# A stationary matmul form rewritten as three 256-column products a step, in a one-core encoder layer

## The chip, the cores and the metric

The kernel runs on one core of one Trainium2 chip. The metric is the device time of one execution in microseconds; lower is better. Engines are named as in the profile: PE is TensorE (matmuls), PEld its weight loads, DVE VectorE, ACT ScalarE, POOL GpSimd and SP SyncE, which here issues nearly all DMAs.

## The reference

One layer of an encoder on 256 tokens of width 2048, in float32:

```
h = rmsnorm(x, g_mix)
proj = einsum('bsd,de->bse', h, w_in)
q_a, k_a, v_a, q_r, f_fwd, f_bwd, i_r, g_r, gate_a, gate_r = split_columns(proj)
...
y_attn = einsum('bse,ed->bsd', bidirectional_gqa(q_a, k_a, v_a), w_o_attn)
o_r = hgrn2_bidirectional(q_r, f_fwd, f_bwd, i_r, g_r, lb, g_hgrn)
y_hgrn = einsum('bse,ed->bsd', o_r, w_o_hgrn)
mixed = sigmoid(gate_a) * y_attn + sigmoid(gate_r) * y_hgrn
x = x + einsum('bsd,de->bse', mixed, w_out)
h = rmsnorm(x, g_mlp)
u = square(relu(einsum('bsd,df->bsf', h, w_up)))
x = x + einsum('bsf,fd->bsd', u, w_down)
ple_gate = sigmoid(einsum('bsd,de->bse', rmsnorm(x, g_ple), w_ple_gate))
x = x + ple_gate * einsum('bsc,cd->bsd', p, w_ple)
return rmsnorm(x, g_final)
```

The attention has 16 query and 4 key heads of 128, with a norm and a rotation of queries and keys. The second branch is a gated linear recurrence with 16 heads, in both directions: `q_r` passes through a SiLU, `f_fwd` and `f_bwd` through a sigmoid. The hidden width of the MLP is 8192.

## The kernel before

**Precision.** Every large product is made of three: an operand is split into a rounded part hi and a remainder lo, both of type float32r, and hi x hi, hi x lo and lo x hi are summed in PSUM. For the weights, `prep_half` makes hi on ACT (line 112) and lo on DVE (line 113), half a tile of 128x1024 at a time. The activations lie in SBUF as `[128, 8, 2, 256]` tiles: for each 128-row block `k` of the inner dimension first the 256 tokens of hi, then those of lo. `xs(X, k)` is such a block, `[128, 2, 256]`.

**Weights.** All weights stream through in a fixed list, `order`, as tiles of 1 MB. `next_w` hands out the next tile, and puts the load of the tile two ahead on SP's queue and the split of the tile one ahead on ACT and DVE.

**Two forms of product.** `gemm_mov` has the activations stationary and the weights moving, 512 columns a product (line 207); it serves most projections. `gemm_st` has the weights stationary and the activations moving, so that results come out transposed; it serves the recurrence's `q_r`, `f_fwd` and `f_bwd` (48 tiles of 128 output features) and the MLP's up-projection (64). It works on two output tiles at once, `e` = 0 and 1, each with a PSUM tile of 512 columns, over 16 blocks `k`. For each `k` the weights' hi part meets both parts of the activations in one product of 512 columns (line 181), and the lo part meets the hi part of the activations in one of 256 (line 184), which adds onto the first 256 columns. The PSUM tile then holds two partial results side by side, and `merge` adds them: ACT copies the second half to SBUF (line 189), DVE adds the first half to it (line 190). What follows reads that sum: a SiLU for `q`, a sigmoid for each forget gate (line 617), and in the MLP the square of the ReLU (line 699).

**Order of the work.** Smaller chains (attention, the scan of the recurrence, the transposes of results) are Python generators. `tick` advances a clock by the time that each group of products is expected to take, and when it reaches a generator's due time, the generator's next piece is put between the large products. So `yield 7.0` means: go on after 7 us of large products. `attend` begins with `heads_T`, which squares each head of the projected queries (line 398), normalizes and rotates them (the last addition on line 414), waits for `pause`, transposes them on TensorE (line 421) and splits the result into `qT` (lines 424 and 425); then come the scores (line 449), the transposes of the probabilities (line 480) and the products with the values (line 469). In the scan, ACT copies keys (line 527) for products on line 535. The engines' queues run in order.

**Start.** SP loads the first quarter of `x` in two pieces of 256 KB, each followed by half of the first weight tile (lines 291 and 292), and then the other quarters and tiles in turn. ACT and DVE split them (lines 303 to 309), and the first large products follow.

Of the kernel before, what the change touches and what calls it, by code (L numbers as in the profile page):

```python
# [7 lines left out]
AF = mybir.ActivationFunctionType  # L8
ALU = mybir.AluOpType
# [3 lines left out]
P = 128  # L13
D = 2048
S = 256
KT = D // P
# [10 lines left out]
def build(tc, xT, xtok, pT, gains, gfin_in, ropet, ident_in, masks_in, ghg_in, lb_in,  # L27
# [41 lines left out]
    with contextlib.ExitStack() as es:  # L69
# [14 lines left out]
        def nm(s):  # L84
            cnt[0] += 1
            return f"{s}_{cnt[0]}"
# [4 lines left out]
        def gps():  # L91
            return psg.tile([P, 512], F32, tag="g", name=nm("g"))
# [66 lines left out]
        def wsl(w, k, n):  # L159
            per = 1024 // n  # L160
            t = w[k // per]
            o = (k % per) * n
            return t[:, o:o + n]
# [5 lines left out]
        def gemm_st(arr, b, X, last=None):  # L169


            ps = [gps() for _ in range(2)]
            for c in range(2):
                his, los = next_w((arr, b + c))
                for kk in range(KT // 2):
                    k = KT // 2 * c + kk
                    if k == 12 and last:
                        last()
                    x = xs(X, k)
                    for e in range(2):  # L180
                        pe.matmul(ps[e], wsl(his, 2 * kk + e, P), x, start=k == 0, stop=False)  # L181
                    tick(0.33)
                    for e in range(2):
                        pe.matmul(ps[e][:, :S], wsl(los, 2 * kk + e, P), x[:, 0, :], start=False, stop=k == KT - 1)  # L184
                    tick(0.33)
            return ps

        def merge(ps, z):
            act.activation(z, ps[:, S:], AF.Copy)
            dve.tensor_tensor(z, ps[:, :S], z, ALU.add)  # L190
            return z

        def gemm_mov(arr, j, X, last=None, stagger=False):

# [91 lines left out]
        dve.memset(nhalf, -0.5)  # L286
        act.dma_start(gn, gains)
        raws[0] = wraw.tile([P, 2048], F32, tag="raw", bufs=3, name=nm("raw"))
        for a in range(2):
            w2 = slice(1024 * a, 1024 * a + 1024)  # L290
            sp.dma_start(xf[:, 2 * a:2 * a + 2], xT[:, 2 * a:2 * a + 2])
            sp.dma_start(raws[0][:, w2], w_mov[order[0][1:]][:, w2])
        for i in range(1, 4):
            sp.dma_start(xf[:, 4 * i:4 * i + 4], xT[:, 4 * i:4 * i + 4])
# [144 lines left out]
        SC = HD ** -0.5  # L439

        def attend(j, ps):
            qT = yield from heads_T(ps, 0, "qT", 7.0 if j else 10.0)
            probs, pts = {}, {}
            for i in range(6):
                if i < 4:
                    sc = mps()
                    for t in range(NT):
                        for n, (a, b) in enumerate(TERMS):
                            pe.matmul(sc[:, t * S:(t + 1) * S], qT[:, i, a, t * P:(t + 1) * P], kT[:, j, b],  # L449
                                      start=n == 0, stop=n == 2)  # L450
                    mx = t1([P, NT], "mx", 2)
                    dve.tensor_reduce(mx, sc.rearrange("p (t s) -> p t s", t=NT), AX.X, ALU.max)
                    dve.tensor_scalar(mx, mx, -SC, None, ALU.mult)
                    pr = com.tile([P, NT, S], F32, tag="yb", bufs=2, name=nm("pr"))
                    sm = t1([P, NT], "sm", 2)
                    for t in range(NT):
                        act.activation(pr[:, t], sc[:, t * S:(t + 1) * S], AF.Exp, bias=mx[:, t:t + 1], scale=SC,
                                       accum_out=sm[:, t:t + 1])
                    dve.reciprocal(sm, sm)
                    for t in range(NT):  # L460
                        dve.tensor_scalar(pr[:, t], pr[:, t], sm[:, t:t + 1], None, ALU.mult)
                    probs[i] = pr
                    yield 1.5
                if 0 <= i - 2 < 4:
                    pt = pts.pop(i - 2)
                    av = mps()
                    for s in range(NT):
                        for n, (a, b) in enumerate(TERMS):
                            pe.matmul(av[:, :S], va[:, s, a, j * HD:(j + 1) * HD], pt[:, s, b],  # L469
                                      start=s == n == 0, stop=s == NT - 1 and n == 2)  # L470
                    o = xs(OA, 4 * j + i - 2)
                    act.activation(o[:, 0, :], av[:, :S], AF.Copy)
                    dve.tensor_tensor(o[:, 1, :], av[:, :S], o[:, 0, :], ALU.subtract)
                    yield 1.5
                if 0 <= i - 1 < 4:
                    pr = probs.pop(i - 1)
                    tp = mps()
                    for s in range(NT):
                        for t in range(NT):
                            pe.transpose(tp[:, s * S + t * P:s * S + (t + 1) * P], pr[:, t, s * P:(s + 1) * P], ident)  # L480
                    pt = t1([P, NT, 2, S], "pt", 1, F32R)
                    tv = tp.rearrange("p (s t) -> p s t", s=NT)
                    act.activation(pt[:, :, 0], tv, AF.Copy)
                    dve.tensor_tensor(pt[:, :, 1], tv, pt[:, :, 0], ALU.subtract)
                    pts[i - 1] = pt
                yield 3.0
# [24 lines left out]
        def scan_head(h, q, T, vi, gg):  # L511
# [16 lines left out]
                return kc  # L528

            kc = keys(1)  # L530
            yield 7.0
            for li, L in enumerate(LEVELS):
                pl = mps()
                for t in range(NT):
# [54 lines left out]
        for j in range(4):  # L589
            ps = proj(f"i{j}", Hm) if j else ps_i0  # L590
            vi = t2([P, NT, 512], "vi")
            for t in range(NT):
                act.activation(vi[:, t], ps[t], AF.Copy)
            ps = proj(f"g{j}", Hm)
            gg = t2([P, NT, 512], "gg")
            for t in range(NT):
                act.activation(gg[:, t], ps[t], AF.Sigmoid)
                dve.tensor_tensor(gg[:, t], ps[t], gg[:, t], ALU.mult)
                g4 = gg[:, t].rearrange("p (h v) -> p h v", h=4)
                pool.tensor_tensor(g4, g4, ghg.unsqueeze(1).to_broadcast([P, 4, HD]), ALU.mult)  # L600
            pend = []
            for h in range(4 * j, 4 * j + 4):
                for a in range(3):
                    if not pend:
                        pend = gemm_st("st", 3 * h + a, Hm)
                    ps = pend.pop(0)
                    if a == 0:
                        q = t2([P, S], "q")
                        sg = t2([P, S], "sg")
                        merge(ps, q)  # L610
                        act.activation(sg, q, AF.Sigmoid)
                        dve.tensor_tensor(q, q, sg, ALU.mult)
                        T = t2([P, 2, S], "T1")
                        continue
                    d = a - 1
                    merge(ps, T[:, d])
                    act.activation(T[:, d], T[:, d], AF.Sigmoid)
                    dve.tensor_scalar(T[:, d], T[:, d], oml[:, d, h:h + 1], low[:, d, h:h + 1], ALU.mult, ALU.add)  # L618
                weave(scan_head(h, q, T, vi, gg))

# [56 lines left out]
        for step in MLP:  # L677
            c = int(step[1])
            if step[0] == "u":
                pend = []  # L680
                for f in range(16):
                    if not pend:
                        pend = gemm_st("up", c * 16 + f, H1, last=flush if c == f == 0 else None)
                    ps = pend.pop(0)
                    if c == f == 0:
                        st3.close()
                        ph4, st4 = open_pool("ph4", side="right")

                        def t4(shape, tag, bufs=2, dt=F32):
                            return ph4.tile(shape, dt, tag=tag, bufs=bufs, name=nm(tag))  # L690

                        row_r(0)
                        dve.tensor_tensor(r1s, rr[0], rr[0], ALU.mult)
                        UA = [bigt(F32R, [P, 8, 2, S]) for _ in range(2)]
                        UB = [t4([P, 8, 2, S], f"UB{i}", 1, F32R) for i in range(2)]
                        t4([P, 120], "pad", 1)
                    r = merge(ps, t4([P, S], "r"))
                    uu = t4([P, S], "uu")
                    dve.scalar_tensor_tensor(uu, r, 0.0, r, ALU.max, ALU.mult)
                    u = xs(UA if c % 2 == 0 else UB, f)  # L700
                    act.activation(u[:, 0, :], uu, AF.Copy)
                    dve.tensor_tensor(u[:, 1, :], uu, u[:, 0, :], ALU.subtract)
                continue
# [161 lines left out]
```

## Time and profile before

| | |
|---|---|
| median of 3 runs | 1979.24 us (1978.99 to 1980.14) |
| the profiled execution | 1979.2 us |
| its span in the trace | 1977.3 us |
| TensorE busy | 1955.2 us, 99% |
| VectorE busy | 1227.8 us, 62% |
| ScalarE busy | 950.6 us, 48% |
| DMA | 358.59 MB, 181 GB/s on average |

The span is the time from the first to the last instruction of the program; the execution's own time has 1.9 us more. The ends of matmuls are modelled in the trace, and successive matmuls overlap, so what a product costs is read from start to start.

### The profile page before, as it was taken

The numbers are of one execution on the slowest core, as the hardware profiler recorded it, in microseconds if no ns is written. First come the engines' busy times: TensorE is split into PE (matmuls) and PEld (weight loads), VectorE is DVE, ScalarE is ACT, GpSimd is POOL, SyncE is SP. The second block draws the span as 40 slices with busy tenths as digits, with TensorE's granted clock in tenths as the row PEclk, the third lists the DMA queues.
The fourth block names the chain that finished last, engine by engine and source line by source line (L and its number), as shares of the span: only waits on it lengthen the run. The fifth ranks groups of instructions, "written<-read, shape, count | busy, mean of one in ns | idle before, by whom it ended". The sixth has DMA issues, their size and how long they took to land.

```text
span 1977.3 us, 25896 instructions
## 1 busy us (share of the span) xinstructions
PE 1955.2 (99%) x9996; PEld 1659.1 (84%) x9996; DVE 1227.8 (62%) x1756; ACT 950.6 (48%) x1512; POOL 109.6 (6%) x161
## 2 busy tenths in 40 slices
PE   8999999999999999999999999999999999999998
PEld 6788888888888888888888888888888888888886
DVE  6877687686785884545545566665466455545555
ACT  6676554454554553434434454443344344434544
POOL 0000021110210110000000000000000000000001
PEclk9999999999999999999999999999999999999999
DMA  8534444544444445555565555555555555555552
GB/s 332 181 132 146 149 158 145 183 146 158 171 145 157 168 147 175 190 194 189 192 234 197 192 175 189 190 192 191 192 192 192 192 192 192 192 192 190 203 197 113
DMA packets 51676, 358.59 MB, mean 181 GB/s; under 512 B 5984, under 2 KB 6240, under 8 KB 9056
## 3 DMA queue, kind: packets, MB, share of 16 engines
q1 hardware_dynamic: 50832, 355.85, 50.3%
q8 instruction: 79, 1.29, 0.2%
q10 hardware_dynamic: 720, 1.08, 0.1%
q14 instruction: 45, 0.37, 0.1%
HBM read 354.81 MB, written 2.10 MB: 180 GB/s over the span
## 4 chain that ended last, share of the span: by engine, by line
PE 92%; DVE 1%; ACT 1%; issue 1%; POOLq 0%; POOL 0%; ACTq 0%; DVEq 0%
PE g L207 55%; PE g L181 20%; PE g L184 10%; PE m L535 3%; PE m L469 1%; PE g L732 1%; PE m L238 1%; PE m L449 1%; PE m L570 0%; PE m L569 0%; PE m L480 0%; PE m L555 0%; ACT hi L112 0%; DVE lo L113 0%; PE m L561 0%
## 5 line engine op out<-in xcount | busy, mean ns | idle before, releaser
L113 DVE TENSOR_TENSOR lo<-raw,hi 128x1024 fp32r<-128x1024 f32 x658 | 805.1, 1243 | 634.8 <-ACT hi L112 600.1
L112 ACT ACTIVATE hi<-raw 128x1024 fp32r<-128x1024 f32 x658 | 677.8, 1055 | 795.6 <-PE g L207 461.1
L207 PE MATMUL g<-hi,big 128*128 128x512 f32 (+1 forms) x2720 | 665.6, 391 | 8.0 <-ACT hi L303 8.0
L207 PEld LDWEIGHTS g<-hi,big 128*128 128x128 f32 x2720 | 501.0, 189 | 106.6 <-ACT hi L303 8.7
L181 PE MATMUL g<-big,hi 128*128 128x512 f32 x1792 | 565.9, 397 | 0.0
L184 PEld LDWEIGHTS g<-big,lo 128*128 128x128 f32 x1792 | 333.8, 188 | 75.5
L184 PE MATMUL g<-big,lo 128*128 128x256 f32 x1792 | 357.4, 280 | 0.0
L207 PE MATMUL g<-lo,big 128*128 128x512 f32 (+1 forms) x1360 | 342.6, 390 | 0.0
L207 PEld LDWEIGHTS g<-lo,big 128*128 128x128 f32 x1360 | 251.0, 188 | 49.8
L181 PEld LDWEIGHTS g<-big,hi 128*128 128x128 f32 x1792 | 274.0, 189 | 0.5
L207 PE MATMUL g<-hi,UB 128*128 128x512 f32 x512 | 122.1, 390 | 0.0
L207 PEld LDWEIGHTS g<-hi,UB 128*128 128x128 f32 x512 | 95.8, 188 | 19.7
L535 PEld LDWEIGHTS m<-QQ,kc 128*128 128x128 f32 x448 | 66.0, 190 | 10.6 <-ACT kc L527 2.7
L527 ACT ACTIVATE kc<-KK 128x256 f32<-128x256 f32 x112 | 47.8, 434 | 56.3 <-PE m L535 30.3
L535 PE MATMUL m<-QQ,kc 128*128 128x128 f32 x448 | 72.9, 286 | 0.9 <-ACT kc L527 0.9
L319 POOL TENSOR_TENSOR c<-c,c 128x2 f32<-128x2 f32 (+1 forms) x5 | 3.2, 640 | 1178.3 <-DVE c L663 1137.7
L207 PE MATMUL g<-lo,UB 128*128 128x512 f32 x256 | 64.1, 390 | 0.0
L549 POOL TENSOR_TENSOR T<-T 128x256 f32<-128x256 f32 (+2 forms) x96 | 48.5, 505 | 257.2 <-DVE T L618 135.9
L207 PE MATMUL g<-hi,MX 128*128 128x512 f32 x256 | 61.7, 391 | 0.0
L542 DVE TENSOR_TENSOR QQ<-QQ,T 128x256 f32<-128x256 f32 x112 | 50.9, 454 | 9.4 <-PE m L535 8.1
L207 PEld LDWEIGHTS g<-lo,UB 128*128 128x128 f32 x256 | 47.8, 188 | 9.8
L207 PEld LDWEIGHTS g<-hi,MX 128*128 128x128 f32 x256 | 47.8, 188 | 9.7
(150 smaller groups left out, 1071.7 us busy)
## 6 DMA issues: line engine op xcount, KB each, us to landing
raw<-w_mov SPq DMA_DIRECT2D x87, 1024.0 KB, 4.8
raw<-w_up SPq DMA_DIRECT2D x64, 1024.0 KB, 4.8
raw<-w_dn SPq DMA_DIRECT2D x64, 1024.0 KB, 4.8
raw<-w_st SPq DMA_DIRECT2D x48, 1024.0 KB, 4.8
raw<-w_oa SPq DMA_DIRECT2D x16, 1024.0 KB, 4.8
raw<-w_oh SPq DMA_DIRECT2D x16, 1024.0 KB, 4.7
raw<-w_out SPq DMA_DIRECT2D x16, 1024.0 KB, 4.7
raw<-w_pg SPq DMA_DIRECT2D x16, 1024.0 KB, 4.7
```

Of the source, the lines that this page charges most:

```text
L112: act.activation(hi, sl, AF.Copy)
L113: dve.tensor_tensor(lo, sl, hi, ALU.subtract)
L181: pe.matmul(ps[e], wsl(his, 2 * kk + e, P), x, start=k == 0, stop=False)
L184: pe.matmul(ps[e][:, :S], wsl(los, 2 * kk + e, P), x[:, 0, :], start=False, stop=k == KT - 1)
L207: last_mm[0] = pe.matmul(dst, xs(X, k)[:, a, t * P:(t + 1) * P], wsl(ws, kk, 512)[:, cols], start=k == 0 and a == 0 and ws is w[0], stop=k ...
L238: pe.transpose(tp[:, a * S + t * P:a * S + (t + 1) * P], srcs[t][:, o:o + P], ident)
L449: pe.matmul(sc[:, t * S:(t + 1) * S], qT[:, i, a, t * P:(t + 1) * P], kT[:, j, b], start=n == 0, stop=n == 2)
L469: pe.matmul(av[:, :S], va[:, s, a, j * HD:(j + 1) * HD], pt[:, s, b], start=s == n == 0, stop=s == NT - 1 and n == 2)
L527: act.activation(kc.rearrange("p (n a b) -> p n a b", a=2, b=L), merged(KK, 0, L, S // (2 * L)), AF.Copy)
L535: pe.matmul(pl[:, t * P:(t + 1) * P], kc[:, t * P:(t + 1) * P], merged(QQ, t * P, L, P // (2 * L)), start=True, stop=True)
L542: dve.tensor_tensor(qv, qv, view(T, nb + 1, [[2, nb // 2], [-(nb + 1), 2], [0, L]]), ALU.mult)
L549: pool.tensor_tensor(Tn, view(T, 0, [[nb, 2], [2, nb // 2]]), view(T, 1, [[nb, 2], [2, nb // 2]]), ALU.mult)
```

## The change

In `gemm_st` the 512-column product of each step becomes two of 256, and all three products of a step write the same 256 columns of PSUM. `merge` goes: the SiLU, the sigmoids and the ReLU read PSUM directly, and so do the products behind them. The ticks become three of 0.22 instead of two of 0.33 a step. The first quarter of `x` is loaded in one DMA of 512 KB, ahead of the two halves of the first weight tile. Two pauses of the generators differ: the first query group's goes from 10 to 7, the scan's first from 7.0 to 7.5.

```diff
         def gemm_st(arr, b, X, last=None):
...
-            ps = [gps() for _ in range(2)]
+            ps = [gps()[:, :S] for _ in range(2)]
...
                     x = xs(X, k)
-                    for e in range(2):
-                        pe.matmul(ps[e], wsl(his, 2 * kk + e, P), x, start=k == 0, stop=False)
-                    tick(0.33)
-                    for e in range(2):
-                        pe.matmul(ps[e][:, :S], wsl(los, 2 * kk + e, P), x[:, 0, :], start=False, stop=k == KT - 1)
-                    tick(0.33)
+                    for n, (ws, a) in enumerate(((his, 0), (his, 1), (los, 0))):
+                        for e in range(2):
+                            pe.matmul(ps[e], wsl(ws, 2 * kk + e, P), x[:, a, :], start=k == 0 and n == 0,
+                                      stop=k == KT - 1 and n == 2)
+                        tick(0.22)
             return ps
-
-        def merge(ps, z):
-            act.activation(z, ps[:, S:], AF.Copy)
-            dve.tensor_tensor(z, ps[:, :S], z, ALU.add)
-            return z
...
         raws[0] = wraw.tile([P, 2048], F32, tag="raw", bufs=3, name=nm("raw"))
+        sp.dma_start(xf[:, 0:4], xT[:, 0:4])
         for a in range(2):
             w2 = slice(1024 * a, 1024 * a + 1024)
-            sp.dma_start(xf[:, 2 * a:2 * a + 2], xT[:, 2 * a:2 * a + 2])
             sp.dma_start(raws[0][:, w2], w_mov[order[0][1:]][:, w2])
...
-            qT = yield from heads_T(ps, 0, "qT", 7.0 if j else 10.0)
+            qT = yield from heads_T(ps, 0, "qT", 7.0)
...
             kc = keys(1)
-            yield 7.0
+            yield 7.5
...
-                        merge(ps, q)
-                        act.activation(sg, q, AF.Sigmoid)
-                        dve.tensor_tensor(q, q, sg, ALU.mult)
+                        act.activation(sg, ps, AF.Sigmoid)
+                        dve.tensor_tensor(q, ps, sg, ALU.mult)
...
-                    merge(ps, T[:, d])
-                    act.activation(T[:, d], T[:, d], AF.Sigmoid)
+                    act.activation(T[:, d], ps, AF.Sigmoid)
...
-                    r = merge(ps, t4([P, S], "r"))
+                    r = t4([P, S], "r")
+                    act.activation(r, ps, AF.Relu)
                     uu = t4([P, S], "uu")
-                    dve.scalar_tensor_tensor(uu, r, 0.0, r, ALU.max, ALU.mult)
+                    dve.tensor_tensor(uu, ps, r, ALU.mult)
```

The rows below are from the order in which the built programs hold each engine's instructions: line, operation, output<-inputs, size of the output for a product and of the transfer for a DMA. In the changed kernel the same lines have other numbers (182 for the stationary products, 201 for line 207, 415 for line 421, 392 and 400 for lines 398 and 406).

TensorE at the first `gemm_st` of the program, first step and the beginning of the second, before (`big` is the activations, `hi` and `lo` the weights):

```order
L181 MATMUL g_2158<-big_558,hi_2119 128x512
L181 MATMUL g_2159<-big_558,hi_2119 128x512
L184 MATMUL g_2158<-big_558,lo_2120 128x256
L184 MATMUL g_2159<-big_558,lo_2120 128x256
L181 MATMUL g_2158<-big_558,hi_2119 128x512
```

and in the changed kernel:

```order
L182 MATMUL g_2157<-big_557,hi_2118 128x256
L182 MATMUL g_2158<-big_557,hi_2118 128x256
L182 MATMUL g_2157<-big_557,hi_2118 128x256
L182 MATMUL g_2158<-big_557,hi_2118 128x256
L182 MATMUL g_2157<-big_557,lo_2119 128x256
L182 MATMUL g_2158<-big_557,lo_2119 128x256
```

A step has six matmuls where it had four; TensorE's whole list grows by 1792 matmuls, and each has a weight load of its own.

SP at the start of the program, before:

```order
L291 DMA big_85<-xT 128x512
L292 DMA raw_90<-w_mov 128x1024
L291 DMA big_85<-xT 128x512
L292 DMA raw_90<-w_mov 128x1024
L294 DMA big_85<-xT 128x1024
L105 DMA raw_96<-w_mov 128x2048
```

and in the changed kernel:

```order
L283 DMA big_85<-xT 128x1024
L286 DMA raw_90<-w_mov 128x1024 x2
L288 DMA big_85<-xT 128x1024
L105 DMA raw_95<-w_mov 128x2048
L288 DMA big_85<-xT 128x1024
```

The first quarter of `x` stands whole ahead of both weight halves; what follows is in the same order.

TensorE around the first transposes of the first query group (`c` is the identity, `za` the rotated queries; `big_86` and `big_87` are blocks 0 to 7 and 8 to 15 of the activations), before:

```order
L207 MATMUL g_672<-hi_755,big_87 128x512
L207 MATMUL g_673<-hi_755,big_87 128x512
L207 MATMUL g_672<-hi_755,big_87 128x512
L207 MATMUL g_673<-hi_755,big_87 128x512
L421 MATMUL m_813<-c_77,za_704 128x128 x4
L207 MATMUL g_672<-hi_759,big_87 128x512
```

and in the changed kernel:

```order
L201 MATMUL g_671<-lo_676,big_86 128x512
L201 MATMUL g_672<-lo_676,big_86 128x512
L415 MATMUL m_781<-c_77,za_703 128x128 x4
L201 MATMUL g_671<-lo_676,big_86 128x512
L201 MATMUL g_672<-lo_676,big_86 128x512
L201 MATMUL g_671<-lo_680,big_86 128x512
```

Counted over the whole order, the first four transposes stand behind 330 large products instead of 340, the second four behind 348 instead of 352.

ACT at the same place, the end of the eight squares (`scr`) of that query group, the two weight copies (`hi`) and the normalized heads (`zn`), before:

```order
L398 ACTIVATE scr_690,ss_689<-g_497,c_145 128x128
L112 ACTIVATE hi_755<-raw_674 128x1024
L112 ACTIVATE hi_759<-raw_674 128x1024
L406 ACTIVATE zn_699<-g_497,rs_695 128x128 x4
L398 ACTIVATE scr_710,ss_709<-g_498,c_145 128x128
L277 ACTIVATE big_559<-big_85 128x4x256
```

and in the changed kernel:

```order
L392 ACTIVATE scr_709,ss_708<-g_497,c_144 128x128
L112 ACTIVATE hi_754<-raw_673 128x1024
L112 ACTIVATE hi_758<-raw_673 128x1024
L400 ACTIVATE zn_698<-g_496,rs_694 128x128 x4
L400 ACTIVATE zn_718<-g_497,rs_714 128x128 x4
L271 ACTIVATE big_558<-big_85 128x4x256
```

The last square of the second token tile moves ahead of the weight copies, and the two groups of normalized heads now stand together. On DVE, the split of the first transposes into `qT` (line 425), which stood ahead of the second addition on line 414, stands behind it.

## Rows read from the trace of the kernel before

**Rows 1.** The page's head, and busy time and share of the span.

```profile
span 1977.3 us, 25896 instructions
...
PE 1955.2 (99%) x9996; PEld 1659.1 (84%) x9996; DVE 1227.8 (62%) x1756; ACT 950.6 (48%) x1512; POOL 109.6 (6%) x161
```

**Rows 2.** The page's chain that ended last, shares by line.

```profile
PE g L207 55%; PE g L181 20%; PE g L184 10%; PE m L535 3%; PE m L469 1%; PE g L732 1%; PE m L238 1%; PE m L449 1%; PE m L570 0%; PE m L569 0%; PE m L480 0%; PE m L555 0%; ACT hi L112 0%; DVE lo L113 0%; PE m L561 0%
```

**Rows 3.** Groups by line and shape: busy us, mean ns | idle before.

```profile
L181 PE MATMUL g<-big,hi 128*128 128x512 f32 x1792 | 565.9, 397 | 0.0
...
L184 PE MATMUL g<-big,lo 128*128 128x256 f32 x1792 | 357.4, 280 | 0.0
...
L699 DVE SCALAR_TENSOR_TENSOR uu<-r 128x256 f32<-128x256 f32 x64 | 24.0, 417 | 0.0
L190 DVE TENSOR_TENSOR r<-g,r 128x256 f32<-128x256 f32 x64 | 23.9, 416 | 0.0
```

**Rows 4.** TensorE's waits over the span: us in total, times, longest.

```profile
PE m L421 <- DVE za L414: 2.3, 2, 2.0
...
PE m L535 <- ACT kc L527: 0.9, 4, 0.2
```

**Rows 5.** Timeline of TensorE, up-projection: start, length of the merged row, count.

```profile
1196.00 0.63 PE L181 MATMUL g<-big,hi 128*128 128x512 f32 x2
1196.47 0.39 PE L184 MATMUL g<-big,lo 128*128 128x256 f32 x2
1196.70 0.63 PE L181 MATMUL g<-big,hi 128*128 128x512 f32 x2
...
1207.15 0.63 PE L181 MATMUL g<-big,hi 128*128 128x512 f32 x2
```

**Rows 6.** Timeline of TensorE, last projection: 16 + 8 and 8 + 4 products between rows.

```profile
1939.17 3.79 PE L207 MATMUL g<-hi,big 128*128 128x512 f32 x16
...
1944.61 4.17 PE L207 MATMUL g<-hi,big 128*128 128x512 f32 x24
...
1963.00 1.12 PE L207 MATMUL g<-hi,big 128*128 128x256 f32 x8
...
1965.88 1.12 PE L207 MATMUL g<-hi,big 128*128 128x256 f32 x8
```

**Rows 7.** Timeline of TensorE, a group of scores in the attention.

```profile
125.01 0.88 PE L449 MATMUL m<-kT,qT 128*128 128x256 f32 x6
125.72 0.63 PE L207 MATMUL g<-lo,big 128*128 128x512 f32 x2
```

**Rows 8.** Timeline of all engines, start: [idle before <-what ended it].

```profile
4.03 0.62 DVE L304 TENSOR_SCALAR big<-big,c 128x256 fp32r<-128x256 f32 x2 [3.16 <-DMA c<-gains]
...
5.86 1.15 ACT L303 ACTIVATE hi<-raw 128x512 fp32r<-128x512 f32 x2 [3.40 <-DMA raw<-w_mov]
...
6.54 2.08 PE L207 MATMUL g<-hi,big 128*128 128x512 f32 x4 [6.54 <-ACT hi L303]
7.84 0.62 DVE L304 TENSOR_SCALAR big<-big,c 128x256 fp32r<-128x256 f32 x2 [2.40 <-DMA big<-xT]
...
9.39 1.15 ACT L303 ACTIVATE hi<-raw 128x512 fp32r<-128x512 f32 x2 [2.38 <-DMA raw<-w_mov]
...
10.08 5.49 PE L207 MATMUL g<-hi,big 128*128 128x512 f32 x12 [1.46 <-ACT hi L303]
...
15.36 2.06 PE L207 MATMUL g<-lo,big 128*128 128x512 f32 x8
```

**Rows 9.** Timeline of all engines, rotated queries of the first group and their transposes.

```profile
89.21 0.69 DVE L414 TENSOR_TENSOR za<-za,zb 128x512 f32<-128x512 f32 x1
...
90.49 0.60 PE L421 MATMUL m<-c,za 128*128 128x128 f32 x4
...
95.02 0.68 DVE L414 TENSOR_TENSOR za<-za,zb 128x512 f32<-128x512 f32 x1
95.84 0.63 PE L421 MATMUL m<-c,za 128*128 128x128 f32 x4 [1.97 <-DVE za L414]
```

## The prediction

> **What bounds the kernel now.** I read the page first. TensorE is busy 1955.2 of 1977.3 us [rows 1], and the chain that ended last is almost wholly its own matmuls: lines 207, 181 and 184 alone are 85% of the span [rows 2]. So work on another engine counts only where TensorE waits for it. The view of TensorE's waits has little to offer: past the start, 2.3 us for the transposes of the rotated queries and 0.9 us in the scan [rows 4]. A busy TensorE may still be a slow one, since ends of matmuls are modelled; so I went on to the timeline and took times from start to start, which is what a matmul costs in a stream. The reader should see three prices there.
>
> First, the step that the change rewrites, in the MLP's up-projection. A pair of output tiles takes 16 steps of two 512-column and two 256-column products, and the same place of the next pair stands 1207.15 - 1196.00 = 11.15 us later [rows 5]: 0.697 us a step. Second, 512-column products in a long stream: 24 of them in 1944.61 - 1939.17 = 5.44 us, 0.2267 us each [rows 6]. Third, 256-column products in a long stream, which the trace has only in the last projection: 24 in 1965.88 - 1963.00 = 2.88 us, 0.1200 us each [rows 6]. Half the columns do not cost half the time: 2 x 0.1200 - 0.2267 = 0.0133 us is what splitting a product costs, since each half brings a fixed part and a weight load of its own.
>
> **The change part by part.**
>
> *The stationary products.* Lines 181 and 184 ran 1792 times each [rows 3], four products a step, so there are 896 steps. Each now has six products of 256 columns: the columns stay 1536, the products and weight loads grow from four to six, and the order has 1792 more matmuls. At 0.1200 a step takes 0.720 us instead of 0.697, so 896 x 0.0231 = +20.7 us. This is the largest term, and it lies on the chain itself: nothing covers it.
>
> How sure is 0.1200? Three other rows bound it. In the attention six 256-column products in a row take 125.72 - 125.01 = 0.71 us, 0.1183 each [rows 7]; at that the term is +11.8. Inside the step itself the two 256-column products start 1196.70 - 1196.47 = 0.23 us ahead of what follows, 0.115 each [rows 5]; at that the term is (0.690 - 0.697) x 896 = -6. But the two 512-column products beside them take 0.47, more than 2 x 0.2267, so the start of one kind borrows from the other. Give the 512-column products their stream price, and the 256-column ones are left with (0.697 - 0.453) / 2 = 0.1218; at that the term is +30. I take 0.1200, as the only row with long runs of nothing but 256 columns, and keep the ends.
>
> The Trainium skill speaks of the same spacing ("TensorE: Matmul & The Clock Gate", section Back-to-back issue gap): N / 2.4 GHz plus about 2.5 ns, so 109 ns for 256 columns and 216 for 512. By it a split costs 2.5 ns and the term is about +4.5 us, an estimate from that page. The rows here show 120 and 227, a fixed part of some 13 ns, and the measurement decides.
>
> *The additions.* The sum of the two halves of a result is gone: 112 ACT copies and 112 DVE additions before. In the MLP the copy becomes a ReLU of the same size, so ACT does as many there, and DVE loses 64 additions, 23.9 us, while the square on line 699 becomes a plain product read from PSUM, of the same 128x256 [rows 3]. In the scan ACT loses 48 copies and DVE 48 additions. I cost all of this at nothing. What hides it is the next pair's products: results have 11.15 us until the pair after next wants their PSUM tiles, and lines 181 and 184 never show TensorE idle before them [rows 3]. If the cover were gone, the most that could return is the 0.9 us that the scan's first products wait for a key copy [rows 4]; the scan's pause goes from 7.0 to 7.5, which leaves them later and that wait no longer. I take 0, with 0.9 either way.
>
> *The start.* Now the first 256 KB of x are in use at 4.03, half a weight tile at 5.86, the next 256 KB of x at 7.84, the other half tile at 9.39; TensorE runs four products from 6.54, and starts again at 10.08 [rows 8]. In one DMA, x comes whole before the first weights. The extra 256 KB cost between half of the 1.55 us in which a 512 KB half tile followed (9.39 - 7.84), 0.78, and the 1.98 that they took in the old place. So the first weights are in use at 6.6 to 7.8 and the second half at 8.2 to 9.4, against 9.39. The first product starts later, at 7.3 to 8.5, and the second four follow either their weights (8.9 to 10.1, adding the 0.69 from ACT's start to the product) or the first four, which at the start's spacing of (15.36 - 10.08) / 12 = 0.44 us end 1.76 later, at 9.1 to 10.3. That is 1.0 earlier to 0.2 later than 10.08; if the faster spacing then also begins sooner, up to 1 us more. I take -0.9, ends +0.2 and -2.0. SP issues one DMA less, and none is moved past another queue's work.
>
> *The pauses.* The first query group's pause falls from 10 to 7, and the order shows its first transposes ten 512-column products earlier and its second four earlier. Now the first ones start at 90.49, just behind the DVE addition that began at 89.21 and takes 0.7; the second wait 1.97 us, for the addition at 95.02 [rows 9]. If that addition ended no sooner, four products fewer would lie ahead of it and the wait would grow by 4 x 0.2267 = 0.9. But ACT now makes the last square before the two weight copies, not after them, and DVE no longer puts the first transposes' split ahead of the second addition, so that addition should come sooner; at best the whole 1.97 goes. Behind the waiting transposes stand all projection products of TensorE, and the scores. I take -1.0, ends +0.9 and -2.0.
>
> **Sum.** 20.7 + 0 - 0.9 - 1.0 = +18.8 us. The profiled execution took 1979.2 us with 1.9 outside its span, as the median of the runs (1979.24) does, so the forecast is 1998.0 us, 0.95% slower.
>
> **Rivals.**
> 1. *Only columns count.* If the fixed part of the added products hides behind the queue of loads, a step stays 0.697 and the gains stand alone: 1979.2 - 1.9 = 1977.3. The 0.115 inside the step speaks for it [rows 5]; the stream at 0.1200 speaks against it [rows 6]. The skill's page named above would put it near 1982, the same verdict. 9%.
> 2. *Faster.* Every product takes the 0.115 that the 256-column pair shows in place: 1979.2 - 6 - 1.9 = 1971. The point that decides is 0.1158 us a product: below it the step saves over 2 us in all and the sum passes -4. Against it: the neighbours of that pair pay for it. 6%.
> 3. *Weight loads become the limit.* Six loads a step, with less streaming to hide each, leave 0.1218 or more: 1979.2 + 30 - 1.9 = 2007 upward. For it: the step's own remainder. Against it: the 0.1200 stream has a load for each product too. 9%.
>
> **Numbers.** The forecast's own case, 0.118 to 0.121 a product, has 76%. A change of 0.2%, 4 us, is about what a measurement of this kernel can tell from none. Rival 2 alone is faster (6%), rival 1 is the same (9%), the rest is slower (85%). For the range I go down to the 0.1183 rows with all gains at their far ends, 11.8 - 0.9 - 2.0 - 2.0 = +6.9, so 1986, and up halfway to the 0.1218 case with the gains small, +25, so 2004. Left out are rivals 1 and 2 and most of rival 3.
>
> **What would show it.** Right: starts of the 256-column products 0.120 apart over whole pairs, a pair of tiles in 11.5 us instead of 11.15, TensorE still 99% busy and with the same few waits, DVE's busy time down by some 40 us to no effect, the second start of products near 9.1 us, and the wait at the second query transposes smaller. Wrong: a pair in 11.1 us (rivals 1 and 2) or in 11.7 (rival 3); or new idle time of TensorE in front of the up-projection or of the transposes, which would mean that a wait and not the product price sets the result.

## The result and the profile after

The changed kernel takes 1994.58 us (median of 4 runs, 1994.03 to 1995.02) against 1979.12 before: 1.0076 times as long, interval 1.0064 to 1.0088. The profiled execution's span is 1993.2 us, 15.8 more than before.

The page's head, engines and chain that ended last, of the changed kernel:

```profile
span 1993.2 us, 29430 instructions
...
PE 1974.3 (99%) x11788; PEld 1759.2 (88%) x11788; DVE 1191.3 (60%) x1644; ACT 931.6 (47%) x1464; POOL 107.1 (5%) x161
...
PE g L201 58%; PE g L182 31%; PE m L529 3%; PE m L463 1%; PE m L443 1%; PE g L725 1%; PE m L232 1%; PE m L564 0%; PE m L563 0%; PE m L474 0%; ACT hi L112 0%; DVE lo L113 0%; DMA raw<-w_mov 0%; PE m L549 0%; PE m L415 0%
...
```

Against [rows 1] TensorE has 1792 matmuls and as many weight loads more, and is busy 19 us longer; DVE lost 36.5 us of work, ACT 19.0, and nothing came of it. The groups by line and shape show the same from the other side: three times 1792 products of 256 columns, no idle time before any of them, and on DVE a plain product of the size that the old square had [rows 3].

```profile
L182 PE MATMUL g<-big,hi 128*128 128x256 f32 x3584 | 585.7, 285 | 0.0
L182 PE MATMUL g<-big,lo 128*128 128x256 f32 x1792 | 362.9, 284 | 0.0
...
L692 DVE TENSOR_TENSOR uu<-g,r 128x256 f32<-128x256 f32 x64 | 24.0, 416 | 0.0
```

The timeline of TensorE in the up-projection, the counterpart of [rows 5]: one step, and the same place of the next pair of tiles.

```profile
1229.91 0.64 PE L182 MATMUL g<-big,hi 128*128 128x256 f32 x4
1230.39 0.40 PE L182 MATMUL g<-big,lo 128*128 128x256 f32 x2
...
1241.43 0.64 PE L182 MATMUL g<-big,hi 128*128 128x256 f32 x4
```

The next pair comes 11.52 us later, 0.720 a step, where it was 11.15. That is the forecast of 0.1200 a product to the last digit. Compared product by product, the two traces part as follows. Each line gives where the same large product starts:

| place | before, us | after, us | lead gained (-) or lost (+) since the line above |
|---|---|---|---|
| first large product | 6.54 | 7.55 | +1.0 |
| 25th, the second weight tile | 17.26 | 15.96 | -2.3 |
| first product of the second query group, in the attention | 78.70 | 77.43 | 0.0 |
| first stationary product | 227.34 | 222.89 | -3.2 |
| end of the scan stage | 760.60 | 765.23 | +9.1 |
| end of the last up-projection | 1690.56 | 1707.15 | +12.0 |
| last matmul | 1967.20 | 1983.76 | 0.0 |
| end of the span | 1977.34 | 1993.16 | -0.7 |

So the stages with the stationary products cost 21.1 us, 12.0 in the up-projection's 32 pairs and 9.1 in the scan stage's 24, the start gave 1.3 and the attention 3.2.

The start on the timeline, beside [rows 8]: one run of 16 products where there were four, a pause and twelve.

```profile
4.89 1.14 DVE L298 TENSOR_SCALAR big<-big,c 128x256 fp32r<-128x256 f32 x4 [4.02 <-DMA c<-gains]
...
6.86 1.15 ACT L297 ACTIVATE hi<-raw 128x512 fp32r<-128x512 f32 x2 [4.41 <-DMA raw<-w_mov]
7.55 6.74 PE L201 MATMUL g<-hi,big 128*128 128x512 f32 x16 [7.55 <-ACT hi L297]
...
14.13 2.00 PE L201 MATMUL g<-lo,big 128*128 128x512 f32 x8
...
15.96 3.79 PE L201 MATMUL g<-hi,big 128*128 128x512 f32 x16
```

And the transposes of the first query group, beside [rows 9]: the first four now wait for their addition, the second four hardly.

```profile
87.46 0.69 DVE L408 TENSOR_TENSOR za<-za,zb 128x512 f32<-128x512 f32 x1
...
88.20 0.66 PE L415 MATMUL m<-c,za 128*128 128x128 f32 x4 [1.09 <-DVE za L408]
...
92.07 0.69 DVE L408 TENSOR_TENSOR za<-za,zb 128x512 f32<-128x512 f32 x1
...
92.91 0.63 PE L415 MATMUL m<-c,za 128*128 128x128 f32 x4
```

### The profile page after: what moved, and what is told of

Its sections match the earlier page's. It is cut to its first block, busy times and chain, and to the rows that moved or that the text cites. A ratio compares the mean times of both kernels' runs of the same rounds, so it can differ in the third digit from the quotient of the medians.

```text
span 1993.2 us, 29430 instructions
## 1 busy us (share of the span) xinstructions
PE 1974.3 (99%) x11788; PEld 1759.2 (88%) x11788; DVE 1191.3 (60%) x1644; ACT 931.6 (47%) x1464; POOL 107.1 (5%) x161
## 4 chain that ended last, share of the span: by engine, by line
PE 97%; DVE 1%; issue 1%; ACT 1%; DMA 0%; POOL 0%; POOLq 0%; SPq 0%; ACTq 0%; DVEq 0%
PE g L201 58%; PE g L182 31%; PE m L529 3%; PE m L463 1%; PE m L443 1%; PE g L725 1%; PE m L232 1%; PE m L564 0%; PE m L563 0%; PE m L474 0%; ACT hi L112 0%; DVE lo L113 0%; DMA raw<-w_mov 0%; PE m L549 0%; PE m L415 0%
## 5 line engine op out<-in xcount | busy, mean ns | idle before, releaser
L182 PE MATMUL g<-big,hi 128*128 128x256 f32 x3584 | 585.7, 285 | 0.0
L182 PEld LDWEIGHTS g<-big,hi 128*128 128x128 f32 x3584 | 496.5, 192 | 0.5
L182 PE MATMUL g<-big,lo 128*128 128x256 f32 x1792 | 362.9, 284 | 0.0
L182 PEld LDWEIGHTS g<-big,lo 128*128 128x128 f32 x1792 | 279.1, 192 | 0.0
L533 DVE TENSOR_TENSOR KK<-KK,T 128x256 f32<-128x256 f32 x112 | 51.2, 460 | 9.7 <-ACT kc L521 6.3
```

Source lines behind the costliest of these rows:

```text
L182: pe.matmul(ps[e], wsl(ws, 2 * kk + e, P), x[:, a, :], start=k == 0 and n == 0, stop=k == KT - 1 and n == 2)
L533: dve.tensor_tensor(kv, kv, view(T, 1, [[2, nb // 2], [nb - 1, 2], [0, L]]), ALU.mult)
```

## The experiments

The theory after the result: the price of a product of the stationary form is fixed by its columns and its weight load, nothing else in the change costs anything on TensorE's path in the up-projection, and start and pauses gain apart from it. The rivals: additions, accumulation onto the same columns, or the placing by finer ticks share in it. Eight kernels ran, four at a time against the kernel before (1979.49 and 1979.58 us in the two sets). The table gives, in each one's profiled execution, how much earlier (-) or later (+) than in the kernel before the same places as above are reached. One pair of traces does not tell a lead at the 25th product to better than about 1 us: the new products alone and the split with additions kept have the start of the kernel before and stand 0.8 earlier there, the query pause alone has it too and stands 0.3 later.

| kernel | time, us | ratio, interval | 25th product | first stationary product | end of the scan stage | last matmul |
|---|---|---|---|---|---|---|
| the change | 1994.58 | 1.0076, 1.0064 to 1.0088 | -1.3 | -4.5 | +4.6 | +16.6 |
| old products, new start and pauses | 1977.95 | 0.9992, 0.9983 to 1.0001 | -1.9 | -5.1 | -0.7 | -0.7 |
| new products alone | 1997.78 | 1.0089, 1.0075 to 1.0103 | -0.8 | +0.6 | +8.1 | +20.1 |
| start alone | 1976.04 | 0.9983, 0.9974 to 0.9992 | -1.9 | -3.2 | -3.6 | -3.6 |
| query pause alone | 1975.57 | 0.9979, 0.9970 to 0.9988 | +0.3 | -2.2 | -2.6 | -2.6 |
| split with additions kept | 1996.64 | 1.0085, 1.0072 to 1.0099 | -0.8 | -0.9 | +6.4 | +17.3 |
| third product in halves of 128 | 2174.36 | one run | -1.7 | -4.9 | +81.4 | +195.8 |
| old products, start and query pause | 1973.96 | 0.9971, 0.9959 to 0.9982 | -1.4 | -4.6 | -4.6 | -4.6 |
| the change, scan's pause at 7.0 | 1992.56 | 1.0067, 1.0053 to 1.0080 | -2.4 | -5.7 | +1.9 | +13.9 |

### The new products alone

The kernel before with the changed `gemm_st`, its ticks, and the reads from PSUM; start and pauses as they were. The diff is the first and the last part of the change's.

> Only the products, additions and ticks are changed; start and pauses are as before. Theory: 56 pairs at 11.52 instead of 11.15 us, +20.9, so 2000.0 us. Rival (part of the loss is made good inside the scan, where chains got shorter): 1996 to 1998. Rival (weight loads now limit and the start hid it): over 2002.

Measured: 1997.78 us. In the up-projections it loses the same 12.0 us as the change. From the first stationary product to the last matmul it loses 19.5, not 20.9: the scan stage costs it 7.6 where 24 pairs at 0.37 make 8.9. The products' price is shown, and 1.3 of it came back in the scan, so the time is the first rival's. The rival's reason, shorter chains, is not shown: the next kernel keeps the additions and loses 7.3 in the scan stage with 360 of its 384 steps split, in proportion 7.8. The 0.6 us that the new products alone have lost at the first stationary product is a matter of their profiled execution (last section).

### The split with the additions kept

```diff
-                    for e in range(2):
-                        pe.matmul(ps[e], wsl(his, 2 * kk + e, P), x, start=k == 0, stop=False)
+                    for e in range(2):
+                        if k == 0:
+                            pe.matmul(ps[e], wsl(his, 2 * kk + e, P), x, start=True, stop=False)
+                        else:
+                            pe.matmul(ps[e][:, :S], wsl(his, 2 * kk + e, P), x[:, 0, :], start=False, stop=False)
+                    if k:
+                        for e in range(2):
+                            pe.matmul(ps[e][:, S:], wsl(his, 2 * kk + e, P), x[:, 1, :], start=False, stop=False)
```

> The kernel before, with the 512-column product of every step but the first of a tile split into two of 256 that write the two halves of the old PSUM tile; the additions, the start and the pauses are as before. Theory (the split alone costs, 0.0231 us a step): 840 steps, +19.4, so 1998.8 us, with the additions back on ACT and DVE and without effect. Rival (the price comes from adding three products in a row onto the same 256 columns): 1979.4. Rival (the additions that the change removed paid something back): well over 1999.

Measured: 1996.64 us. The timeline of TensorE shows a step of three pairs, 1230.55 - 1229.83 = 0.72 us:

```profile
1229.83 0.40 PE L190 MATMUL g<-big,lo 128*128 128x256 f32 x2
1230.07 0.40 PE L184 MATMUL g<-big,hi 128*128 128x256 f32 x2
1230.31 0.40 PE L187 MATMUL g<-big,hi 128*128 128x256 f32 x2
1230.55 0.40 PE L190 MATMUL g<-big,lo 128*128 128x256 f32 x2
```

So splitting the product costs by itself, and it does not matter that all three products of a step write the same columns: that rival falls. From the first stationary product on it loses 17.3 + 0.9 = 18.2 us with 840 of 896 steps split; in proportion 19.4 for all, where the products without additions lost 19.5. The 112 copies and 112 additions are worth nothing that these runs can tell.

### The third product in halves of 128 columns

```diff
                         for e in range(2):
-                            pe.matmul(ps[e], wsl(ws, 2 * kk + e, P), x[:, a, :], start=k == 0 and n == 0,
-                                      stop=k == KT - 1 and n == 2)
+                            for o, m in ((0, S),) if n < 2 else ((0, P), (P, P)):
+                                pe.matmul(ps[e][:, o:o + m], wsl(ws, 2 * kk + e, P), x[:, a, o:o + m],
+                                          start=k == 0 and n == 0, stop=k == KT - 1 and n == 2 and o == P)
```

> The changed kernel with the third product of each step, the weights' lo part, split once more into two of 128 columns. Theory A (a product costs its columns plus 0.0133 us): 0.067 us a 128-column product, a step 0.747, +24, so 2018 us. Theory B (a product with its own weight load cannot follow the one before in less than about 0.110 us, the spacing of the 128-column products in the scan): a step 0.92, +179, so 2174 us, and 256 columns at 0.120 are already near that floor.

Measured: 2174.36 us in the one run, where theory B said 2174. The timeline of TensorE in the up-projection, and then busy times of a stretch of it, followed by a stretch of the changed kernel's:

```profile
1429.74 0.69 PE L183 MATMUL g<-big,hi 128*128 128x256 f32 x4
1430.26 0.56 PE L183 MATMUL g<-big,lo 128*128 128x128 f32 x4
1430.66 0.69 PE L183 MATMUL g<-big,hi 128*128 128x256 f32 x4
```

```profile
core 0: us, PE busy (x) PEld busy (x) DVE busy (x) ACT busy (x) POOL busy (x), PEclk, DMA share, GB/s
1430.00:1435.00 5.00, 5.00 (x46) 5.00 (x45) 2.53 (x4) 1.61 (x3) 0.00 (x0) 1.00 0.31 126
```

```profile
1230.00:1235.00 5.00, 5.00 (x44) 5.00 (x43) 1.69 (x3) 2.53 (x4) 0.00 (x0) 1.00 0.61 210
```

A step of eight products takes 1430.66 - 1429.74 = 0.92 us, 0.115 apart on average (the counts in brackets take in matmuls that lie across a window's ends). Four products of 256 columns at 0.120 leave 0.44 for four of 128, 0.110 each, where columns and a fixed 0.0133 alone would make 0.067. The three sizes fit a product that costs the larger of two things: its columns plus about 0.013 us, or about 0.110. At 512 columns the second is far away, at 256 it is 0.01 away, at 128 it rules. That theory B names the weight load as the cause is not shown by this: every product of these kernels has a load of its own, and the busy time of the loads does not tell the cases apart, since it has no gap (5.00 of 5.00 us) in the changed kernel's stream of 256 columns either.

### The start alone, the query pause alone

Each is one line or two of the change's diff on the kernel before.

> Only the first quarter of x comes in one DMA. Theory: the first product starts 1.0 us later, the 25th 1.3 us earlier, and all that follows keeps it: 1977.8 us. Rival (the lead is lost at the first wait for the rotated queries, since their chain runs on ACT and DVE and not on TensorE): the 25th product 1.3 earlier, but the time within 0.3 of 1979.1.

> Only the first query group's pause is 7 instead of 10. Theory: the wait of the second four query transposes shrinks from 1.97 to about 1, the later wait of 1.02 for the split of the probabilities goes, and the small ones around them: 3.0 us less, 1976.1. Rival (the gain in the attention came from the earlier start): 1979.1 within 0.5. Rival (the wait only moves, to the scores behind the transposes): waits of TensorE in the attention still near 3.3 us in sum, 1979.

Measured: 1976.04 and 1975.57 us. The start did more than its theory: a lead of 1.9 at the 25th product, and another 1.4 gained in the attention, against the rival that would have it lost there. The pause alone gained 2.5 from the 25th product to the first stationary one, against the rival of the earlier start, and TensorE's waits in the attention sum to 1.7 us where they were 3.3, against the rival of the moved wait. These waits, first of the start alone, then of the pause alone (us in total, times, longest; of before in [rows 4]):

```profile
PE m L421 <- DVE za L414: 1.1, 1, 1.1
PE m L469 <- DVE pt L484: 1.0, 1, 1.0
```

```profile
PE m L421 <- DVE za L414: 1.7, 2, 0.9
PE m L535 <- ACT kc L527: 0.9, 4, 0.2
```

Both shrink the same wait for the rotated queries, 2.3 us before. The start does it through the order on DVE and ACT, which differs from before's there too though no pause was touched: with the start alone ACT makes the normalized heads of both token tiles in one go, with the pause alone the last square of the second tile still stands behind those of the first, as before. First the start alone, then the pause alone:

```profile
81.89 2.21 ACT L406 ACTIVATE zn<-g,rs 128x128 f32<-128x128 f32 x8
```

```profile
84.17 1.14 ACT L406 ACTIVATE zn<-g,rs 128x128 f32<-128x128 f32 x4
...
85.18 0.39 ACT L398 ACTIVATE scr<-g,c 128x128 f32<-128x128 f32 x1
```

So the order on ACT that the prediction lists under the pauses came with the start. The pause also ends the wait of the products with the values, for the split of the probabilities (line 469), which is 1.0 before as well:

```profile
PE m L469 <- DVE pt L484: 1.0, 1, 1.0
```

Together they gain 3.3 in the attention, not the 3.9 of their sum, because they share the wait for the rotated queries. What is left with both is 1.1 us at the first transposes.

### The old products with the new start and pauses

> The stationary products, the additions and their ticks are as before; the one-DMA start and both changed pauses stay. Theory (the loss of the change is 896 steps times 0.0231 us and nothing else; start and pauses give back 1.3 and about 3.1 us): 1979.1 - 4.4 = 1974.7 us, an up-projection pair back at 11.15 us. Rival (start and pauses gain only because the finer ticks of the new products place the small chains better): no gain, 1979. Rival (the missing additions paid for part of the products' price): above 1975 by what they gave.

Measured: 1977.95 us, ratio 0.9992 with an interval that holds 1. The theory's figure fell. The lead at the first stationary product is 5.1 us, as large as with the change, so the rival of the finer ticks falls too. But 4.4 of it goes in the scan stage, about 1.1 for each of the four groups of heads. The time alone would fit the second rival, with the additions back and costing 3 us; but nothing is lost in the up-projections, where 64 of the 112 are. TensorE's wait for the scan's key copies is 2.3 us in 8 where it was 0.9 in 4:

```profile
PE m L535 <- ACT kc L527: 2.3, 8, 0.3
```

The other suspect in the scan was its pause of 7.5, costed at nothing in the prediction. Two kernels test it: the same one with the scan's pause at 7.0, and the change with it at 7.0.

> The kernel before with the one-DMA start and the first query group's pause of 7; products, additions and the scan's pause of 7.0 as before. Theory (the scan's pause of 7.5 took back 4.4 us in the version that had it beside the old products): the lead of 5.1 us at the first stationary product is kept to the end, 1974.3 us. Rival (the loss in the scan came from entering it earlier, with the same pause): 1978, as that version.

> The changed kernel with the scan's first pause back at 7.0. Theory (a longer pause delays the scan's chain against the products that follow it): the scan stage 1.5 us shorter, as in the version with the products alone, so 1993.1 us. Rival (7.5 fits the finer ticks and the shorter chain): the same 1994.6 or slower.

Measured: 1973.96 us, the fastest version of the study, 0.9971 of the kernel before (0.9959 to 0.9982), with its lead of 4.6 at the first stationary product kept to the last matmul, though the additions are there: the rival that charged them falls. The change at 7.0 takes 1992.56 us. So the longer pause costs 4.4 us beside the old products, and beside the new ones 9.1 - 7.5 = 1.5 in the scan stage. The waits of the weight loads in the scan stage (us in total, times, longest) show where, first of the old products with the pause of 7.0 and with 7.5:

```profile
PEld m L535 <- ACT kc L527: 2.7, 4, 0.7
```

```profile
PEld m L535 <- ACT kc L527: 7.9, 12, 0.8
```

and then of the changed kernel with 7.0 and with 7.5 (its lines 529, 521, 536 and 555 are 535, 527, 542 and 561 of the kernel before):

```profile
PEld m L555 <- DVE QQ L536: 2.5, 4, 0.6
```

```profile
PEld m L529 <- ACT kc L521: 3.3, 8, 0.4
PEld m L555 <- DVE QQ L536: 1.1, 4, 0.3
```

With either form the longer pause makes the loads for the scan's products with the keys (line 535) wait longer for ACT's copies, 5.2 us longer beside the old products and 3.3 beside the new ones. Beside the new ones it also takes 1.4 off the wait for DVE's line 536, which the old ones do not show. That leaves 5.2 against 1.9 us, near the ratio of the two costs, 4.4 and 1.5, so this accounts for most of the difference. Why the key copies come later with the longer pause is open.

## Why the prediction was right, and where its terms were off

**The stationary products: right, in mechanism and size.** +20.7 was forecast and 21.1 measured between the first stationary product and the end of the last up-projection; the step is 0.720. The up-projection alone is the clean case, 12.0 for 512 steps where 11.8 was due; that the scan stage came out close as well was luck (below). Taking the 256-column stream of the last projection as the price, against 0.115, 0.1183 and 0.1218, was the choice that decided, and the pair of 11.52 us shows it. The step in place is no guide to its parts: its 0.115 and its 0.1218 were both wrong. The split with additions kept shows that the price is the split's own, the split into 128 how it goes with the width.

**"Only columns count" and "faster"** fall with the step. **"Weight loads become the limit"** fell in its price, 0.1218 or more a product at 256 columns. One halving further a product does cost far more than its columns, 0.110; that the load is what sets this is argued and not shown.

**The Trainium skill's rule on the spacing** gave 109 ns for 256 columns and 216 for 512 ("TensorE: Matmul & The Clock Gate", section Back-to-back issue gap). The section calls this the gap of isolated matmuls, and gives about 81 ns at 128 columns and 131 at 512 for a stream of weight loads and matmuls. The traces agree with neither: 256 columns stand 120 apart in the changed kernel's up-projection, and 128 and 512 cost 110 and 227. The estimate of +4.5 made from that page of the Trainium skill would have been less than a quarter of what was measured.

**The additions: right at nothing.** DVE's 36.5 us less and ACT's 19.0 changed no time that the runs can tell.

**The scan's pause: not nothing.** It was costed at 0 with 0.9 either way, for "that wait no longer". The weight loads' wait for the key copies grew with it instead, and it cost 1.5 us here. The whole scan stage still came out at 9.1 against the 8.9 of its 24 pairs, because with the pause at 7.0 the new products cost that stage only 7.6 and 7.5, in the kernel of the new products alone and in the change at 7.0. Two errors of opposite sign cancelled.

**The start: -0.9 forecast, -1.3 measured,** and -1.4 to -2.4 in the five other kernels with the one DMA. Over all traces the 25th product starts at 14.88 to 15.96 us with one DMA and at 16.43 to 17.55 with two, 1.4 apart in the mean. The first weights came into use at 6.86, inside 6.6 to 7.8, and the first product at 7.55; the four first products were no longer followed by a wait, as said.

**The attention: -1.0 forecast, -3.2 measured; the term that was mis-sized most.** The step that failed is the pause's: it looked at one wait of 1.97 us and halved it. The first four transposes wait 1.09 now and the second four barely, so of that wait about 0.9 went. The rest came from places that the sum left out: the wait of 1.0 for the split of the probabilities, a row of the view that the prediction passed over when it named 2.3 and 0.9 as all there is past the start, and which the pause alone removes; the other 0.3 of those 2.3, at the second query group; and about 1.0 in delays too short for the view, by starts most of them at the products with the values. And part of the mechanism was laid to the wrong edit: the earlier second addition owes the order on ACT to the start, which alone gained 1.4 in the attention, where the sum had nothing for it.

With -0.7 at the tail the sum was +15.8 instead of +18.8, and the time 3.4 us under the forecast. The time from the last matmul to the end is 9.3 to 10.2 us over the traces of this study, also between kernels whose tail is the same code, so that 0.7 is put down to no cause.

## What to carry to other kernels

On an engine that is 99% busy, price a changed instruction by the start-to-start spacing of its own form in a long stream, not by its share of a mixed one and not by its columns: here products of 512, 256 and 128 columns cost 0.227, 0.120 and 0.110 us, so one wide product is worth some additions elsewhere, if those are hidden. A change that takes work from engines that nobody waits for pays nothing, and it is best undone when it costs the busy one. Edits that come bundled should be timed apart: of four here two gained, two lost, and the two that gain make 0.9971 of the time.

## What was not expected of the hardware

In the profiled execution of the new products alone, the wait of 1.98 us for the second query transposes, of the same length as in [rows 9], was followed by products at half the speed. The timeline, and the stretches around it with the granted clock (the column before the DMA share):

```profile
95.04 0.63 PE L415 MATMUL m<-c,za 128*128 128x128 f32 x4 [1.98 <-DVE za L408]
95.42 3.27 PE L201 MATMUL g<-lo,big 128*128 128x512 f32 x8
98.49 1.51 PE L201 MATMUL g<-hi,big 128*128 128x512 f32 x4
```

```profile
92.00:96.00 4.00, 2.02 (x12) 1.45 (x11) 2.89 (x5) 2.31 (x3) 0.00 (x0) 1.00 0.65 207
96.00:99.40 3.40, 3.40 (x10) 2.63 (x9) 1.82 (x2) 0.30 (x1) 0.00 (x0) 0.50 0.16 65
99.40:104.00 4.60, 4.60 (x25) 3.91 (x24) 2.09 (x4) 1.41 (x2) 0.00 (x0) 1.00 0.66 221
```

and the middle stretch in the kernel before:

```profile
96.00:99.40 3.40, 3.40 (x19) 2.89 (x19) 1.91 (x2) 0.60 (x1) 0.00 (x0) 1.00 0.41 169
```

The granted clock fell from 2.4 to 1.2 GHz after that wait, and eight products took 98.49 - 95.42 = 3.07 us where 1.81 was due; over the whole stretch it cost about 1.6 us. The kernel before and the split with additions kept, with a wait of 1.97 us in the same place, kept their clock in their profiled executions. So a wait of this size can cost nearly twice its length or not, and a wait removed, as by the pause, is worth more than its row says in the executions in which this happens; how many these are was not measured.

The spacing of that stretch, 0.43 us a product, shows at the start too (the clock column reads 1.00 there, so this goes by the spacing alone). In the traces with the one-DMA start the first 16 products run in one go, and take 14.13 - 7.55 = 6.58 us in the changed kernel, 13.59 - 7.81 = 5.78 in the one with the start alone, and 13.07 - 7.72 = 5.35 in the change with the scan's pause at 7.0:

```profile
7.81 5.95 PE L207 MATMUL g<-hi,big 128*128 128x512 f32 x16 [7.81 <-ACT hi L303]
13.59 1.98 PE L207 MATMUL g<-lo,big 128*128 128x512 f32 x8
```

```profile
7.72 5.51 PE L201 MATMUL g<-hi,big 128*128 128x512 f32 x16 [7.72 <-ACT hi L297]
13.07 1.98 PE L201 MATMUL g<-lo,big 128*128 128x512 f32 x8
```

At 0.227 us each 16 would take 3.6, so the slow spacing lasted through much of them and ended at a different moment in each execution. The first product starts at 7.55 to 7.92 in these six traces, so most of what varies in the start's gain on this side is when the slow spacing ends.
